# An 8-byte constant moves into another tile's slot: all later SBUF tiles of the first phase start 32 bytes lower

## The chip, the cores and the metric

One core of one Trainium2 chip runs the kernel. The metric is the device time of one execution in microseconds; the kernel before took 2728.22 us, the median of three runs (2727.66, 2728.22 and 2730.35). One more execution was recorded by the profiler, and all rows below are from it.

## What is computed

One layer of a hybrid decoder, on 4096 tokens of width 1024, in float32:

```
h    = rms_norm(x, norm_g)
u_lru, q, k, v, g_lr, q_xa, gate = split(h @ w_in)
y_lru = rg_lru(causal_conv4(u_lru), ...)          # gated linear recurrence, width 1024
y_gla = gla(q, k, v, g_lr @ w_g2 + b_g, ...)      # chunked linear attention, 4 heads
y_xa  = cross_attention(q_xa, rms_norm(mem) @ w_mem_kv)   # 256 memory tokens
y    = concat(y_lru, y_gla, y_xa) * silu(gate)    # width 2048
out  = rms_norm(x + y @ w_out, final_norm_g)
```

`b_g` is the bias of the decay logits of the linear attention; its negative, two numbers per partition, is the constant `nbg` of this case.

## The kernel before, in words

Matmuls need about float32 accuracy and are run in the type float32r. Each operand is split into a high and a low part of 4 bytes per element, and one product becomes three matmuls (`mm3`, lines 73 to 76): high by high, high by low, low by high. In `nc.tensor.matmul(o, a, b)` the second argument `a` is the stationary operand, a block of 128 by 128 that a weight load (PEld in the profile) brings into TensorE, and `b` is the moving operand, which streams past it. The page names them the other way round: `gate<-hh,whi` has `hh` moving and `whi` stationary.

Phase 1 works through the tokens in 4 blocks of 1024, each in two units of 512. `prep_gen` brings the normed activations of a unit into `hh` and `hl` (high and low part). `load_group` (line 102) loads a group of weights by DMA into `raw`, splits it on ScalarE (`whi`, line 110) and VectorE (`wlo`, line 111). `proj` (line 115) makes a projection: 8 slices of the contraction, three matmuls each, 24 matmuls of 512 columns, with the weights stationary and the activations moving. Names of the results are `gate`, `u`, `q` and `k`. The values `vp` (lines 475 to 477) are projected the other way: activations stationary, weights moving, 256 columns (272 where the low-rank decay factors ride along, with the first pair of heads). Between projections stand short pieces of the mixers: gates of the recurrence (`pr`, `pi`, lines 347 and 348), scores and output of the cross-attention (`sp`, lines 411 to 413; `ov`), and chunked attention in plain float32 (`pa`, `pk`, `pkv`, `po`, `pt`). Their steps are written as generators, one step per projection, so TensorE has projections to run while ScalarE and VectorE make its next operands. Every engine takes its instructions in the written order.

Phase 2 (from line 747) multiplies the gated outputs, read back from DRAM and split into `yh` and `yl` (stationary), by the output weights `wohi` and `wolo` (moving, 512 columns), adds the residual and norms. These are the matmuls `out`.

Where a tile lies in SBUF: pools are laid one behind the other in the order in which they are opened, each tile in its pool in the order in which it is made, and a tile's size per partition is rounded up to a multiple of 32 bytes. `cst` (constants of both phases, `hgn` among them), `small` and `hp` (`hh`, `hl`, later the first output weights) come first. Then follow the pools of phase 1: `c1` (constants, `nbg` among them), `xp`, `wp` (weights), `wk` and `wk1` (work tiles). When phase 1 ends its pools are closed, and those of phase 2 start where `c1` had started.

```
    hgn = cst.tile([P, 4], F32, name="hgn")                         # 16 bytes in a slot of 32
    nbg = c1.tile([P, 2], F32, name="nbg")                          # 8 bytes in a slot of 32
    ...
            nc.scalar.activation(out=rl[:, usl(u)], in_=z, func=AF.Relu, scale=-1.0, bias=nbg[:, p:p + 1])
```

Of the kernel before, what the change touches and what calls it, by code (L numbers as in the profile page):

```python
# [9 lines left out]
F32 = mybir.dt.float32  # L10
# [4 lines left out]
ALU = mybir.AluOpType  # L15
# [4 lines left out]
P = 128  # L20
# [6 lines left out]
EPS = 1e-6  # L27
LW = 1152

# columns of the packed per-channel parameters  # L30
C_CW, C_CB, C_BA, C_BI, C_LAM, C_BG, C_GN, C_NG, C_MG = 0, 32, 40, 48, 56, 64, 66, 70, 78
NPRM = 86
VW = 272
# [3 lines left out]
def hybrid_layer(ctx: ExitStack, tc: tile.TileContext, x, x_t, mem, mem_t, final_g,  # L37
                 w_lru, w_v0, w_oth, w_g2, w_mem, w_out, prm, out):
    nc = tc.nc
    T = x.shape[0]  # L40
# [21 lines left out]
    def col(c, n=1):  # L62
        return prm_sb[:, c:c + n]

    def rstd_of(ss, n, cols, tag, eng=None):
        """(ss/n + eps)^-0.5 on a [128, cols] tile."""
        ms = small.tile([P, cols], F32, tag=tag + "m", name=tag + "m")
        (eng or nc.gpsimd).tensor_scalar(out=ms, in0=ss, scalar1=1.0 / n, scalar2=EPS, op0=ALU.mult, op1=ALU.add)
        r = small.tile([P, cols], F32, tag=tag + "r", name=tag + "r")
        nc.gpsimd.tensor_tensor(out=r, in0=ms, in1=mhalf[:, :cols], op=ALU.pow)  # L70
        return r
# [11 lines left out]
    wk = p1.enter_context(tc.tile_pool(name="wk", bufs=2))  # L83
    wk1 = p1.enter_context(tc.tile_pool(name="wk1", bufs=1))

    # Work that waits for other engines is traced one step per projection tile, so that
    # the tensor engine has projections to run while its next operands are made.
    active = []

    def tick():  # L90
# [22 lines left out]
        return hi, lo  # L113

    def proj(o, wg, i, h, n=UNIT):
        """o[128 channels, n tokens] of channel tile i of a weight group."""
        hi, lo = wg
        hh, hl = h
        for kt in range(KT):
            s = slice(kt * P, (kt + 1) * P)  # L120
            mm3(o, hi[:, i, s], lo[:, i, s], hh[:, kt, :n], hl[:, kt, :n], kt == 0, kt == KT - 1)

    def prep_gen(src, src_t, tok0, n, c_g, hsel, spare=None, lean=False):
        """Normed activations of n token tiles, channel-major and split: x^T * g * rstd."""
        w = n * P
        nk = D // w
        t = slice(tok0 * P, tok0 * P + w)
        pend = []

        def load(i):  # L130
            xt = big(spare[i % len(spare)]) if lean else xp.tile([P, D], F32, tag="xt", name="xt", bufs=2)
            xt = xt.rearrange("p (k t) -> p k t", t=w)
            nc.sync.dma_start(out=xt, in_=src_t[i * nk * P:(i + 1) * nk * P, t].rearrange("(k p) t -> p k t", p=P))
            pend.append(xt)
        if lean:
            # the sums of squares from the transposed tiles alone
            for i in range(KT // nk):
                load(i)
            sq = xp.tile([P, D], F32, tag="x", name="sqs")[:, :w]
            for i in range(KT // nk):  # L140
                for k in range(nk):
                    if i + k == 0:
                        nc.scalar.activation(out=sq, in_=pend[i][:, k], func=AF.Square)
                        continue
                    s2 = wk.tile([P, w], F32, tag="t2", name="s2")
                    nc.scalar.activation(out=s2, in_=pend[i][:, k], func=AF.Square)
                    nc.vector.tensor_tensor(out=sq, in0=sq, in1=s2, op=ALU.add)
            ss = aux("ss")[:, :n]
            for c in range(n):
                nc.tensor.matmul(ss[:, c:c + 1], sq[:, c * P:(c + 1) * P], ones[:, 0:1], start=True, stop=True)  # L150
        else:
            ss = small.tile([P, n], F32, tag="xss", name="xss", bufs=3)
            for c in range(n):
                xr = big(spare[c % len(spare)]) if spare else xp.tile([P, D], F32, tag="x", name="x")
                nc.sync.dma_start(out=xr, in_=src[(tok0 + c) * P:(tok0 + c + 1) * P, :])
                junk = wk.tile([P, D], BF16, tag="t2", name="junk")
                nc.scalar.activation(out=junk, in_=xr, func=AF.Square, accum_out=ss[:, c:c + 1])
        r = rstd_of(ss, D, n, "x", nc.vector if lean else nc.gpsimd)
        yield 1
        if not lean:  # L160
            for i in range(2):
                load(i)
        yield 1
        pr = aux("rb")
        for c in range(n):
            nc.tensor.transpose(out=pr[:, c * P:(c + 1) * P], in_=r[:, c:c + 1].broadcast_to([P, P]),
                                identity=ident)
        rb = xp.tile([P, w], F32, tag="rb", name="rb")
        nc.scalar.copy(out=rb, in_=pr[:, :w])
        hh = hp.tile([P, KT, UNIT], F32R, tag="hh", name="hh")  # L170
        hl = hp.tile([P, KT, UNIT], F32R, tag="hl", name="hl")
        hsel((hh, hl))
        for i in range(KT // nk):
            xt = pend.pop(0)
            for k in range(nk):
                kt = i * nk + k
                nc.vector.scalar_tensor_tensor(out=xt[:, k], in0=xt[:, k], scalar=col(c_g + kt), in1=rb,
                                               op0=ALU.mult, op1=ALU.mult)
                nc.scalar.copy(out=hh[:, kt, :w], in_=xt[:, k])
                nc.vector.tensor_tensor(out=hl[:, kt, :w], in0=xt[:, k], in1=hh.bitcast(F32)[:, kt, :w],  # L180
                                        op=ALU.subtract)
            if not lean and i + 2 < KT // nk:
                load(i + 2)
            yield 1
# [19 lines left out]
    wm.append(load_group([w_mem[2], w_mem[3]], 1024))  # L204
    pending = [prep_x(0, 0), prep_x(0, 1)]

# [1 line left out]
    cmask = c1.tile([P, P], F32, name="cmask")  # L208
    make_upper_triangular(nc, cmask)
    attm = []  # L210
# [16 lines left out]
        nc.gpsimd.memset(t, 0.0)  # L227
        s_st.append(t)

    # c4 = 4 softplus(-lam) = 4 * (max(-lam, 0) + log1p(exp(-|lam|))), log1p(e) = 2 artanh(e / (2 + e))  # L230
    lam = col(C_LAM, 8)
    sc = cst.tile([P, 8, 8], F32, name="sc")
    e_ = sc[:, 0, :]
# [24 lines left out]
    nc.gpsimd.tensor_scalar(out=nba, in0=col(C_BA, 8), scalar1=-1.0, scalar2=None, op0=ALU.mult)  # L258
    hbi = cst.tile([P, 8], F32, name="hbi")
    nc.gpsimd.tensor_scalar(out=hbi, in0=col(C_BI, 8), scalar1=0.5, scalar2=None, op0=ALU.mult)  # L260
    hgn = cst.tile([P, 4], F32, name="hgn")
    nc.gpsimd.tensor_scalar(out=hgn, in0=col(C_GN, 4), scalar1=0.5, scalar2=None, op0=ALU.mult)
    nbg = c1.tile([P, 2], F32, name="nbg")
    nc.gpsimd.tensor_scalar(out=nbg, in0=col(C_BG, 2), scalar1=-1.0, scalar2=None, op0=ALU.mult)

    # low-rank decay path: the second factor stacked as [hi, lo, hi] to meet [hi, hi, lo] of the first
    gt = c1.tile([P, 4, 96], F32, name="gt")
    nc.gpsimd.memset(gt, 0.0)
    w2raw = wk1.tile([96, 256], F32, tag="ulo", name="w2raw")
# [2 lines left out]
    nc.scalar.copy(out=w2, in_=w2raw)  # L272
    nc.vector.tensor_tensor(out=w2[32:64, :], in0=w2raw[32:64, :], in1=w2.bitcast(F32)[32:64, :], op=ALU.subtract)

# [1 line left out]
    km_hi = c1.tile([P, 4, 256], F32R, name="km_hi")  # L276
    km_lo = c1.tile([P, 4, 256], F32R, name="km_lo")
    vm_hi = c1.tile([P, 2, 512], F32R, name="vm_hi")
# [5 lines left out]
    def silu_gate(wg, i, h, sg, u):  # L284
# [1 line left out]
        proj(g, wg, i, h)  # L286

        def post():
            # 2 silu(g) = (1 + tanh(g / 2)) g; what it multiplies carries the half
            nc.scalar.activation(out=sg[:, usl(u)], in_=g, func=AF.Tanh, scale=0.5)  # L290
            nc.vector.scalar_tensor_tensor(out=sg[:, usl(u)], in0=sg[:, usl(u)], scalar=1.0, in1=g,
                                           op0=ALU.add, op1=ALU.mult)
# [5 lines left out]
                          in_=y.rearrange("p (s t) -> p s t", t=P))  # L298

    class Group:  # L300
        """A pair of projection tiles; unit(u) yields after each projection."""

        def __init__(self, b, j, wg):
            self.b, self.j, self.wg = b, j, wg
# [5 lines left out]
    class Lru(Group):  # L310
        def setup(self):
            self.sg = self.rr = None
            # the last units are not held up for one another
            self.eager = self.b == nblk - 1 and self.j >= 6

        def unit(self, u, h):
# [10 lines left out]
        def post(self, u, o):  # L327
# [26 lines left out]
            if u < NU - 1 and not self.eager:  # L354
# [1 line left out]
            yield 1  # L356
            yield 1
            w = usl(u) if self.eager else slice(0, BLK)
            # 2 sigmoid(z) = exp(min(z, 0)) (1 + tanh(|z| / 2)), as exact in the lower tail as in the upper
            nc.scalar.activation(out=rr[:, w], in_=rr[:, w], func=AF.Tanh, scale=0.5)  # L360
            nc.scalar.activation(out=aa[:, w], in_=aa[:, w], func=AF.Exp, scale=-1.0)
            nc.vector.scalar_tensor_tensor(out=rr[:, w], in0=rr[:, w], scalar=1.0, in1=aa[:, w],
                                           op0=ALU.add, op1=ALU.mult)
            # log a = -c4 * 2 r; 1 - a^2 = tanh(c4 * 2 r) * (1 + a^2)
            nc.scalar.activation(out=aa[:, w], in_=rr[:, w], func=AF.Exp, scale=c4n[:, j:j + 1])
            nc.scalar.activation(out=rr[:, w], in_=rr[:, w], func=AF.Tanh, scale=c4[:, j:j + 1])
            for v in range(NU):
# [82 lines left out]
    gla_lr = {}  # L450

    class GlaV(Group):
        """Values, token-major; with the first pair of heads come the low-rank decay factors."""

        def setup(self):
            gla[self.j].clear()
# [53 lines left out]
                yield 1  # L510

    def gla_decay(p):
        """exp(+-(c - m)) with c the decay summed over 128 tokens and m its value at the midpoint."""
        gr = gla_lr["gr"]
        az, rl = big("r"), big("a")
        for u in range(NU):
# [115 lines left out]
                    store_y(self.b, 8 + 2 * p + hd, sg)  # L632
            yield 1

# [1 line left out]
    kinds = {"L": Lru, "X": Xa, "V": GlaV, "G": GlaG, "Q": GlaQ}  # L636

    def srcs(k, n):
# [16 lines left out]
        if i < len(flat) and i not in loaded:  # L655
            loaded[i] = load_group(*srcs(*flat[i][1:]))

    # memory keys and values, projected while the first tokens are normed
    def mem_post(ct, o):
        if ct < 4:  # L660
            nc.scalar.copy(out=km_hi[:, ct, :], in_=o[:, :256])
# [30 lines left out]
            tick()  # L692
    load_next(1)

    # output weights: the first 8 row tiles take the place of the activations of the last units
    wo = {}

    def wo_split(ct, raw, hi, lo):
# [45 lines left out]
        tick()  # L744
    p1.close()

# [1 line left out]
    yp = ctx.enter_context(tc.tile_pool(name="yp", bufs=2))  # L748
    rp = ctx.enter_context(tc.tile_pool(name="rp", bufs=2))
    w2a = ctx.enter_context(tc.tile_pool(name="w2a", bufs=1))  # L750
# [131 lines left out]
```

## Time and profile before

| | |
|---|---|
| runs | 2727.66, 2728.22, 2730.35 us |
| span of the profiled execution | 2731.1 us |
| TensorE busy (matmul) | 2696.2 us, 99% of the span |
| VectorE, ScalarE busy | 1382.1 us (51%), 1157.5 us (42%) |
| granted TensorE clock, mean | 0.998 of full speed |
| first projection, first matmul of phase 2 | about 62 us, about 2022 us into the span |

The page gives the span, from the first to the last instruction, and no other time of that execution; the span is 2.9 us (0.1%) above the median of the runs. A matmul's duration in the trace holds its way through the pipeline, so neighbours overlap: the pace of TensorE is read from the distance of two starts, not from a duration.

### The profile page before, as it was taken

To read this page: it belongs to the slowest core of one execution; us is meant where nothing else is said; L and a number is where in the kernel's file an instruction comes from. 1 tells how busy PE (TensorE), PEld (TensorE's weight loads), DVE (VectorE), ACT (ScalarE), POOL (GpSimd) and SP (SyncE) were. 2 spreads that over 40 slices of the span, in tenths; PEclk is the share of its full clock that TensorE was granted. 3 is DMA by queue.
4 is the path that set the end of the run, shared out by engine and by line. 5 is a ranking of instruction groups with operands and counts; after the bars stand their busy time and mean duration, and the time that the engine had idled before them with its cause. 6 is when DMAs were issued, how large, how long until landed. Compare 5 with 4: busy or idle time off the path is not lost.

```text
span 2731.1 us, 32855 instructions
## 1 busy us (share of the span) xinstructions
PE 2696.2 (99%) x13338; PEld 2249.0 (82%) x13338; DVE 1382.1 (51%) x2349; ACT 1157.5 (42%) x1802; POOL 88.7 (3%) x197
## 2 busy tenths in 40 slices
PE   7999999999999999999999999999999999999998
PEld 6888888888888878888887888888877888888887
DVE  6466546656664566666455756554573222222221
ACT  6355534644554465356436636543472111111110
POOL 2000000000000000000000000000000000000000
PEclk9999999999999999999999999999999999999999
DMA  8211212331212134112213312121243232222221
GB/s 273 66 59 57 62 58 66 123 104 52 71 54 64 51 118 127 56 58 64 64 49 104 101 51 76 54 70 41 66 164 137 93 106 102 101 93 93 93 93 62
DMA packets 119928, 231.64 MB, mean 85 GB/s; under 512 B 6528, under 2 KB 73184, under 8 KB 115680
## 3 DMA queue, kind: packets, MB, share of 16 engines
q1 hardware_dynamic: 119776, 229.54, 26.0%
q8 instruction: 104, 1.70, 0.3%
q14 instruction: 48, 0.39, 0.0%
HBM read 179.19 MB, written 50.33 MB: 84 GB/s over the span
## 4 chain that ended last, share of the span: by engine, by line
PE 89%; DVE 4%; DMA 4%; ACT 3%; issue 1%; POOL 0%; SPq 0%; DVEq 0%; POOLq 0%; ACTq 0%
PE out L75 8%; PE out L76 8%; PE out L74 8%; PE gate L74 8%; PE gate L75 8%; PE gate L76 8%; PE u L76 4%; PE u L75 4%; PE u L74 4%; PE q L74 3%; PE q L76 3%; PE q L75 3%; DMA x<-in_x 2%; PE vp L477 2%; PE vp L476 2%; PE vp L475 2%
## 5 line engine op out<-in xcount | busy, mean ns | idle before, releaser
L74 PE MATMUL gate<-hh,whi 128*128 128x512 f32 x1024 | 406.9, 397 | 0.0
L76 PE MATMUL gate<-hh,wlo 128*128 128x512 f32 x1024 | 405.0, 396 | 0.0
L75 PE MATMUL gate<-hl,whi 128*128 128x512 f32 x1024 | 405.0, 396 | 0.0
L75 PE MATMUL out<-wolo,yh 128*128 128x512 f32 x1024 | 398.8, 389 | 1.8 <-DVE wolo L706 1.5
L74 PE MATMUL out<-wohi,yh 128*128 128x512 f32 x1024 | 398.1, 389 | 1.0 <-ACT wohi L705 1.0
L76 PE MATMUL out<-wohi,yl 128*128 128x512 f32 x1024 | 398.4, 389 | 0.0
L111 DVE TENSOR_TENSOR wlo<-raw,whi 128x1024 fp32r<-128x1024 f32 (+2 forms) x152 | 191.5, 1281 | 222.0 <-ACT whi L110 185.9
L776 DVE TENSOR_TENSOR xr<-xr,out 128x512 f32<-128x512 f32 x64 | 43.9, 687 | 444.7 <-PE out L76 444.7
L76 PEld LDWEIGHTS gate<-hh,wlo 128*128 128x128 f32 x1024 | 192.3, 188 | 46.5
L74 PEld LDWEIGHTS gate<-hh,whi 128*128 128x128 f32 x1024 | 192.4, 188 | 46.4 <-issue 1.5
L110 ACT CAST whi<-raw 128x1024 fp32r<-128x1024 f32 (+2 forms) x152 | 162.5, 1096 | 157.6 <-PE gate L75 99.5
L75 PEld LDWEIGHTS gate<-hl,whi 128*128 128x128 f32 x1024 | 192.4, 188 | 44.7
L75 PEld LDWEIGHTS out<-wolo,yh 128*128 128x128 f32 x1024 | 192.2, 188 | 43.1 <-DVE wolo L706 2.7
L74 PEld LDWEIGHTS out<-wohi,yh 128*128 128x128 f32 x1024 | 192.1, 188 | 41.9 <-ACT wohi L705 2.0
L76 PEld LDWEIGHTS out<-wohi,yl 128*128 128x128 f32 x1024 | 192.2, 188 | 39.8
L74 PE MATMUL u<-hh,whi 128*128 128x512 f32 x512 | 206.6, 403 | 0.0
L75 PE MATMUL u<-hl,whi 128*128 128x512 f32 x512 | 202.4, 395 | 0.0
L76 PE MATMUL u<-hh,wlo 128*128 128x512 f32 x512 | 202.3, 395 | 0.0
L333 DVE SCALAR_TENSOR_TENSOR uc<-u,prm_sb,uc 128x511 f32<-128x511 f32 (+2 forms) x192 | 143.0, 745 | 75.2 <-ACT uc L330 74.7
L759 ACT CAST yh<-yr 128x2048 fp32r<-128x2048 f32 x32 | 61.2, 1912 | 257.7 <-PE out L75 256.4
L778 ACT ACTIVATE j<-xr 128x512 bf16<-128x512 f32 x64 | 40.0, 625 | 305.0 <-DVE xr L776 305.0
L74 PE MATMUL q<-hh,whi 128*128 128x512 f32 x384 | 152.6, 397 | 0.0
(219 smaller groups left out, 4977.0 us busy)
## 6 DMA issues: line engine op xcount, KB each, us to landing
raw<-in_w_oth SPq DMA_DIRECT2D x72, 512.0 KB, 3.8
raw<-in_w_lru SPq DMA_DIRECT2D x64, 576.0 KB, 3.9
yr<-y_d SPq DMA_DIRECT2D x32, 1024.0 KB, 5.2
xt<-in_x_t SPq DMA_DIRECT2D x32, 512.0 KB, 3.7
y_d<-sg SPq DMA_DIRECT2D x32, 512.0 KB, 3.8
y_d<-i SPq DMA_DIRECT2D x32, 512.0 KB, 3.2
xr<-in_x SPq DMA_DIRECT2D x32, 512.0 KB, 3.5
out<-xr SPq DMA_DIRECT2D x31, 512.0 KB, 4.1
```

The lines of the kernel that those rows point to most:

```text
L74: nc.tensor.matmul(o, w_hi, r_hi, start=start, stop=False)
L75: nc.tensor.matmul(o, w_hi, r_lo, start=False, stop=False)
L76: nc.tensor.matmul(o, w_lo, r_hi, start=False, stop=stop)
L110: nc.scalar.copy(out=hi[:, i, :width], in_=raw[:, :width])
L111: nc.vector.tensor_tensor(out=lo[:, i, :width], in0=raw[:, :width], in1=hi.bitcast(F32)[:, i, :width], op=ALU.subtract)
L333: nc.vector.scalar_tensor_tensor(out=uc[:, d:UNIT], in0=o[:, 0:UNIT - d], scalar=w, in1=uc[:, d:UNIT], op0=ALU.mult, op1=ALU.add)
L475: nc.tensor.matmul(o, hh, wh, start=kt == 0, stop=False)
L476: nc.tensor.matmul(o, hh, wl, start=False, stop=False)
L477: nc.tensor.matmul(o, hl, wh, start=False, stop=kt == KT - 1)
L759: nc.scalar.copy(out=yh, in_=yr)
L776: nc.vector.tensor_tensor(out=xt[:, c], in0=xt[:, c], in1=o[n], op=ALU.add)
L778: nc.scalar.activation(out=junk, in_=xt[:, c], func=AF.Square, accum_out=ss[:, n:n + 1])
```

## The change

`nbg` is no longer a tile of `c1`. `hgn` grows from 4 to 6 numbers per partition (24 bytes, still in its slot of 32), and `nbg` is the last two of them. The readers of `nbg` read the same values from there. Elsewhere the diff only drops comments; line numbers stay.

```
-    hgn = cst.tile([P, 4], F32, name="hgn")
-    nc.gpsimd.tensor_scalar(out=hgn, in0=col(C_GN, 4), scalar1=0.5, scalar2=None, op0=ALU.mult)
-    nbg = c1.tile([P, 2], F32, name="nbg")
+    hgn = cst.tile([P, 6], F32, name="hgn")
+    nc.gpsimd.tensor_scalar(out=hgn[:, 0:4], in0=col(C_GN, 4), scalar1=0.5, scalar2=None, op0=ALU.mult)
+    nbg = hgn[:, 4:6]
     nc.gpsimd.tensor_scalar(out=nbg, in0=col(C_BG, 2), scalar1=-1.0, scalar2=None, op0=ALU.mult)
```

The instructions of all five engines are the same in number, kind and order. What differs is where tiles start. Byte addresses within a partition, and the rest on division by 64:

| tiles | before | rest | after | rest |
|---|---|---|---|---|
| `hh` (two buffers), `hl` (two) | 20928, 37312, 53696, 70080 | 0 | the same | 0 |
| `qz0`, `qz1`, `attm0` to `3`, `s_st0`, `s_st1`, `ident`, `st` | | 0 | the same | 0 |
| `gt`, `w2`, `km_hi`, `km_lo`, `vm_hi`, `vm_lo` | 100832 ... 115680 | 32 | 32 less | 0 |
| `xt`, `rb`, `glr`, `x` | 119776 ... 134112 | 32 | 32 less | 0 |
| `whi` (two), `wlo` (two) | 138208, 147424, 156640, 165856 | 32 | 32 less | 0 |
| `raw`, `sg`, `t2`, `i`, `r`, `a`, `uc`, `ulo`, `uhi` | 175072 ... 227296 | 32 | 32 less | 0 |
| phase 2: `yh`, `yl`, `wohi`, `wolo`, `xr`, ... | 86464 ... 215488 | 0 | the same | 0 |

The slices that matmuls read in these tiles start at multiples of 64 bytes from the tile's start (512 bytes for a block of 128, 1024 and 1088 bytes for the values' weights).

## Rows read from the trace of the kernel before

**Rows 1.** The page: engines' busy time, and the granted clock in 40 slices
```profile
span 2731.1 us, 32855 instructions
PE 2696.2 (99%) x13338; PEld 2249.0 (82%) x13338; DVE 1382.1 (51%) x2349; ACT 1157.5 (42%) x1802; POOL 88.7 (3%) x197
PEclk9999999999999999999999999999999999999999
```

**Rows 2.** Groups by line: output and inputs, form, count | busy us, mean ns | idle us
```profile
L75 PE MATMUL gate<-hl,whi 128*128 128x512 f32 x1024 | 405.0, 396 | 0.0
L75 PE MATMUL u<-hl,whi 128*128 128x512 f32 x512 | 202.4, 395 | 0.0
L75 PE MATMUL q<-hl,whi 128*128 128x512 f32 x384 | 151.8, 395 | 0.0
L75 PE MATMUL k<-hl,whi 128*128 128x512 f32 x128 | 50.6, 396 | 0.0
L76 PE MATMUL out<-wohi,yl 128*128 128x512 f32 x1024 | 398.4, 389 | 0.0
L76 PE MATMUL ov<-phi,vm_lo 128*128 128x512 f32 x64 | 24.9, 390 | 0.0
L476 PE MATMUL vp<-wlo,hh 128*128 128x256 f32 x256 | 71.5, 279 | 0.0
L476 PE MATMUL vp<-wlo,hh 128*128 128x272 f32 x256 | 74.3, 291 | 0.0
L412 PE MATMUL sp<-km_lo,uhi 128*128 128x256 f32 x128 | 35.9, 283 | 0.0
```

**Rows 3.** Timeline, TensorE, projections q and k: start us, duration us, instruction
```profile
366.12 0.40 PE L74 MATMUL q<-hh,whi 128*128 128x512 f32 x1
...
388.28 0.39 PE L76 MATMUL k<-hh,wlo 128*128 128x512 f32 x1
```

**Rows 4.** Timeline, TensorE, phase 2
```profile
2299.65 0.39 PE L74 MATMUL out<-wohi,yh 128*128 128x512 f32 x1
...
2321.86 0.39 PE L76 MATMUL out<-wohi,yl 128*128 128x512 f32 x1
```

**Rows 5.** Windows: us, busy us (count) of each engine, clock, DMA share, GB/s
```profile
660.00:680.00 20.00, 20.00 (x87) 16.14 (x86) 17.27 (x29) 18.04 (x24) 0.00 (x0) 1.00 0.38 113
840.00:860.00 20.00, 20.00 (x87) 16.14 (x86) 3.16 (x4) 3.19 (x5) 0.00 (x0) 1.00 0.23 73
2300.00:2320.00 20.00, 20.00 (x90) 16.57 (x89) 4.87 (x5) 3.25 (x5) 0.73 (x2) 1.00 0.27 98
```

**Rows 6.** Timeline, TensorE, cross-attention output and recurrence gates
```profile
231.30 0.39 PE L75 MATMUL ov<-plo,vm_hi 128*128 128x512 f32 x1
...
233.57 0.39 PE L76 MATMUL pi<-uhi,wlo 128*128 128x512 f32 x1
```

**Rows 7.** Timeline, TensorE, scores of the cross-attention
```profile
197.20 0.28 PE L412 MATMUL sp<-km_lo,uhi 128*128 128x256 f32 x1
...
198.40 0.28 PE L413 MATMUL sp<-km_hi,ulo 128*128 128x256 f32 x1
```

**Rows 8.** Timeline, TensorE, values of 272 columns, then of 256
```profile
73.39 0.29 PE L475 MATMUL vp<-whi,hh 128*128 128x272 f32 x1
...
85.28 0.29 PE L477 MATMUL vp<-whi,hl 128*128 128x272 f32 x1
...
326.45 0.28 PE L475 MATMUL vp<-whi,hh 128*128 128x256 f32 x1
...
343.13 0.28 PE L477 MATMUL vp<-whi,hl 128*128 128x256 f32 x1
```

**Rows 9.** Timeline, TensorE, a wait at the end of a block
```profile
497.28 0.39 PE L411 MATMUL sp<-km_hi,uhi 128*128 128x256 f32 x1 [1.28 <-ACT uhi L403]
```

**Rows 10.** Timeline, ScalarE, sums of squares of the next tokens
```profile
979.34 1.06 ACT L157 ACTIVATE junk<-x 128x1024 bf16<-128x1024 f32 x1 [1.83 <-DMA x<-in_x]
...
984.10 1.06 ACT L157 ACTIVATE junk<-x 128x1024 bf16<-128x1024 f32 x1 [3.60 <-DMA x<-in_x]
```

**Rows 11.** Window at the turn from block 2 to block 3
```profile
1020.00:1060.00 40.00, 39.97 (x229) 34.76 (x228) 38.14 (x65) 28.14 (x48) 0.00 (x0) 1.00 0.50 152
```

**Rows 12.** Groups by line: the same operation on tiles of both phases
```profile
L111 DVE TENSOR_TENSOR wlo<-raw,whi 128x1024 fp32r<-128x1024 f32 x80 | 95.8, 1222 | 84.7 <-ACT whi L110 48.7 <-PE pT L434 35.5
L706 DVE TENSOR_TENSOR wolo<-wraw,wohi 128x1024 fp32r<-128x1024 f32 x8 | 9.8, 1224 | 7.3 <-ACT wohi L705 7.3
L705 ACT CAST wohi<-wraw 128x1024 fp32r<-128x1024 f32 x8 | 8.3, 1044 | 8.4 <-DMA wraw<-in_w_out 8.3
```

## The prediction

> **What bounds the kernel now.** I read the page's engine table first: TensorE is busy for 99% of the span at the full granted clock, VectorE for 51% and ScalarE for 42% [rows 1]. So the time is the number of matmuls times the distance between two starts, plus a few waits. The groups by line give the counts and a first oddity: the same kind of matmul, 512 columns with a full stationary block, takes 395 to 396 ns in a projection of phase 1 and 389 ns in phase 2, and 390 ns in the `ov` of phase 1 [rows 2]. These durations overlap, so I took distances of starts from the timeline.
>
> - Projections `q` and `k`: 96 matmuls in a row, 95 distances from 366.12 to 388.28 us, 22.16 / 95 = 233.3 ns [rows 3].
> - Phase 2: 99 matmuls in a row, 98 distances from 2299.65 to 2321.86, 22.21 / 98 = 226.6 ns [rows 4].
> - `ov`, `pr`, `pi` one behind the other, in phase 1: 10 distances from 231.30 to 233.57, 227 ns [rows 6].
>
> The 6.6 ns between the first and the other two are not disturbance by other engines: two stretches of projections, one with VectorE and ScalarE busy 17.27 and 18.04 of 20 us, the other 3.16 and 3.19, hold the same 87 matmuls, and phase 2 holds 90 [rows 5]. Nor is it the phase, since `ov` to `pi` lie in the middle of phase 1. What differs is the place of the two operands, which the table of addresses in the section on the change gives. In a projection the moving operand (`hh`, `hl`) starts at a multiple of 64 bytes and the stationary one (`whi`, `wlo`) 32 bytes past one. In phase 2 both start at a multiple. In `ov`, `pr` and `pi` both start 32 past one. So, by these rows, 512 columns cost 226.6 ns when both operands have the same rest modulo 64 (a larger power of two up to 256 would fit as well), and 233.3 ns when the rests differ.
>
> With 256 columns the order is the other way round. `sp`, both at rest 32: 10 distances in 1.20 us, 120.0 ns [rows 7]. `vp`, moving at rest 32, stationary at 0: 143 distances in 16.68 us, 116.6 ns; with 272 columns 95 distances in 11.89 us, 125.2 ns [rows 8]. At 2.4 GHz, the granted clock in all these stretches, 512 columns alone are 213.3 ns and 256 are 106.7 ns; equal rests add 13.3 ns to both, unequal ones 19.9 ns to 512 columns and 9.9 ns to 256.
>
> **The change part by part.** No instruction is added, removed or moved. After it every matmul of phase 1 has both operands at rest 0, which is the case of phase 2.
>
> 1. Projections: 3 x (1024 + 512 + 384 + 128) = 6144 matmuls [rows 2], all back to back on the path that sets the end. Each comes 233.3 - 226.6 = 6.6 ns sooner (22.16/95 less 22.21/98): -40.6 us. If rests had no part in it: 0.
> 2. `ov`, `pr`, `pi`: 9 groups of 64, one of them shown [rows 2], 576 matmuls. Settled they already run at 227 ns [rows 6]; those next to a projection are still at its pace. Between 0 and 576 x 6.6 ns = 3.8 us; I take -1, since the group's mean of 390 ns is near the 389 of phase 2.
> 3. Values: 768 matmuls of 256 columns and 768 of 272 (three lines of 256 each [rows 2]). No row shows such a matmul with both at rest 0. The nearest is `sp`, equal rests and 256 columns, at 120.0: +3.4 ns each, +2.6 us; for 272 columns 113.3 + 13.3 = 126.6, +1.4 ns each, +1.1 us. The other end: if the added time grows with the columns, 226.6 x 256/512 = 113.3 and 226.6 x 272/512 = 120.4, that is -2.5 and -3.7 us. I take the first, being the nearer row.
> 4. `sp`: both operands move together, rest 32 to rest 0: 0, as phase 2 and `ov` show for 512 columns. At the other end 113.3 ns, 384 x 6.7 = -2.6 us.
> 5. VectorE, ScalarE, DMA: the same subtraction takes 1222 ns on phase 1's tiles at rest 32 and 1224 ns on phase 2's at rest 0 [rows 12]. I cost them at nothing; TensorE's work covers them anyway.
> 6. Waits that become late. TensorE arrives sooner at places where others set the time. At the end of a block ScalarE stands in its order behind sums of squares that wait for DMA through a single buffer, 4.8 us apart [rows 10], and TensorE waits 1.28 us for it [rows 9]. At the turn of a block VectorE is busy 38.14 of 40 us [rows 11]; what TensorE gains there, some 160 projections x 6.6 ns = 1.1 us, it gives back. With some 20 us in front of the first place (85 matmuls, 0.6 us) this is 1.7 us a turn, three turns: +5 us. It is at least 0; if the stretches that other engines pace are twice as long, +10.
>
> Sum: -40.6 - 1 + 2.6 + 1.1 + 5 = -32.9 us. Against the profiled span 2731.1 that is 2698.2; the runs' median lies 2.9 us below that span, so 2695.3, say 2695 us.
>
> **The rule that speaks against it.** Two kinds of rows say that starts matter to TensorE [rows 3, 4]. The Trainium skill says otherwise in two places. *SBUF — State Buffer*, under "Door 1: The DMA port swizzle", gives SBUF lines of 16 bytes; both layouts start on one. *TensorE: Matmul & The Clock Gate*, under "Step-by-step", says of weight loads: "Loading the next tile's weights doesn't steal SBUF read bandwidth from the running matmul." By these two step 1 would be 0 and the time the one of before, the first of the rivals below. The trace does not agree, as to equal distances: 233.3 against 226.6 ns.
>
> **The rivals.**
>
> - *No change.* The two paces come from something else that is fixed in the program, such as which regions of SBUF the operands lie in (`hh` low, `whi` high), and stay. For it: the cause is inferred from three kinds of pairs. Against: `pr` takes the very tile `whi` as stationary and runs at 227 [rows 6]. Step 3 would go with it: 2728 us.
> - *Short matmuls gain too.* Rest 0 is better than equal rests at 32, and the added time goes with the columns: steps 3 and 4 at their other ends. -40.6 - 1 - 2.5 - 3.7 - 2.6 + 5 = -45.4, less 2.9: 2682.8 us. For it: nothing but that 0/0 at 256 columns is not in the trace. Against: `sp` at 120.0, and 0/0 and 32/32 alike at 512.
> - *Equal rests collide, slower than before.* In the values equal rests are the dearer case, 120.0 against 116.6. If that, 3.4 ns for each stationary block loaded beside a running matmul, is what alignment does in phase 1, and the 226.6 of phase 2 has another cause, then 6144 x 3.4 = +20.9 us and +3.7 for the values: 2728 + 25 = 2753 us. It decides if a projection's distance rises above 233.3 at all. Against: `ov` to `pi`, equal rests, 512 columns, 227.
> - *The change does not do what it says.* `hgn` with 24 bytes still fits its slot of 32, so `hh` stays and all behind `nbg` goes down by 32; I leave it no chance of its own.
>
> **How the numbers follow.** The forecast has 0.70, with its own range of 2689 to 2704 (step 6 between 0 and +10, step 2 between its ends, step 3 as taken). Short matmuls gain too: 0.18. No change: 0.08. Collision: 0.04. The range 2681 to 2706 takes in the forecast and the second rival, with 2 us beyond each, and leaves out the other two and the tails, some 0.15. What a measurement of this kernel can tell from no change is about 0.2%, 5.5 us. Faster by more: the first two, 0.88. Within: 0.08. Slower: 0.04.
>
> **What would show it.** In the profile after, the timeline of `q` and `k` should show 226.6 ns from start to start, and the groups of the projections 389 ns instead of 395 to 396. `vp` should show 120 and 126.6 ns (113.3 and 120.4 for the second rival), `sp` 120.0 as before. The waits of lines 411 and 477 should be a little longer. Phase 2 should begin some 33 us earlier and last as long. The prediction is wrong at its first step if the projections stay at 233.3 ns; it is wrong in step 6 if they go to 226.6 and phase 2 begins less than 25 us earlier.

## Result and profile after

The changed kernel took 2699.27 us, the median of four runs (2698.56 to 2699.65), against 2728.01 for four runs of before: ratio 0.9892, 95% interval [0.9878, 0.9906], 28.7 us less. The forecast was 2695 us. The profiled execution has a span of 2697.9 us and lies 1.75 us below the time of its own run.

The page after, its engine table and the clock, for [rows 1]:

```profile
span 2697.9 us, 32855 instructions
PE 2660.9 (99%) x13338; PEld 2249.6 (83%) x13338; DVE 1381.3 (51%) x2349; ACT 1156.6 (43%) x1802; POOL 92.4 (3%) x197
PEclk9999999999999999999999999999999999999999
```

The instructions are the same in number, the clock is the same, and the work of VectorE and ScalarE is within 1 us of before. Only the busy time of TensorE falls, by 35.3 us. The groups by line, for [rows 2] (busy us, mean ns | idle us):

```profile
L75 PE MATMUL gate<-hl,whi 128*128 128x512 f32 x1024 | 398.6, 389 | 0.0
L75 PE MATMUL u<-hl,whi 128*128 128x512 f32 x512 | 199.6, 390 | 0.0
L75 PE MATMUL q<-hl,whi 128*128 128x512 f32 x384 | 149.7, 390 | 0.0
L75 PE MATMUL k<-hl,whi 128*128 128x512 f32 x128 | 49.8, 389 | 0.0
L76 PE MATMUL out<-wohi,yl 128*128 128x512 f32 x1024 | 398.4, 389 | 0.0
L476 PE MATMUL vp<-wlo,hh 128*128 128x256 f32 x256 | 72.4, 283 | 0.0
L476 PE MATMUL vp<-wlo,hh 128*128 128x272 f32 x256 | 74.6, 292 | 0.0
L111 DVE TENSOR_TENSOR wlo<-raw,whi 128x1024 fp32r<-128x1024 f32 x80 | 95.7, 1222 | 85.9 <-ACT whi L110 51.5 <-PE pT L434 34.1
```

The projections, at 395 to 396 ns before, now take the 389 to 390 of phase 2; the values of 256 columns went up from 279 to 283; VectorE's subtraction, whose three tiles all moved, stays at 1222. The timeline of `q` and `k`, for [rows 3] (start us, duration us):

```profile
360.54 0.39 PE L74 MATMUL q<-hh,whi 128*128 128x512 f32 x1
...
362.62 0.39 PE L74 MATMUL q<-hh,whi 128*128 128x512 f32 x1
...
382.12 0.39 PE L76 MATMUL k<-hh,wlo 128*128 128x512 f32 x1
```

95 distances in 21.58 us are 227.2 ns, where before it was 233.3. The stretch begins right behind a short piece of another kind (`z`): its first 9 distances, up to 362.62, average 232 ns, the other 86 average 226.7. Phase 2 begins 31.9 us earlier, at 1989.64 instead of 2021.59 us:

```profile
1989.64 0.39 PE L74 MATMUL out<-wohi,yh 128*128 128x512 f32 x1
```

And the wait at the end of a block, for [rows 9], with the window at the turn of the block, for [rows 11]:

```profile
489.55 0.39 PE L411 MATMUL sp<-km_hi,uhi 128*128 128x256 f32 x1 [1.73 <-ACT uhi L403]
```
```profile
1005.00:1045.00 40.00, 39.95 (x232) 35.32 (x231) 38.18 (x66) 27.82 (x47) 0.00 (x0) 1.00 0.51 155
```

The wait grew from 1.28 to 1.73 us: TensorE gets there 8.2 us sooner than before, what ScalarE makes for it (`uhi`) only 7.7 us. VectorE is as full at the turn as before.

### The profile page after: what moved, and what is told of

The parts are those of the page before. It is cut to its first block, busy times and chain, and to the rows that moved or that the text cites. A ratio compares the mean times of both kernels' runs of the same rounds, so it can differ in the third digit from the quotient of the medians.

```text
span 2697.9 us, 32855 instructions
## 1 busy us (share of the span) xinstructions
PE 2660.9 (99%) x13338; PEld 2249.6 (83%) x13338; DVE 1381.3 (51%) x2349; ACT 1156.6 (43%) x1802; POOL 92.4 (3%) x197
## 2 busy tenths in 40 slices
DMA packets 119928, 231.64 MB, mean 86 GB/s; under 512 B 6528, under 2 KB 73184, under 8 KB 115680
## 3 DMA queue, kind: packets, MB, share of 16 engines
q1 hardware_dynamic: 119776, 229.54, 26.2%
## 4 chain that ended last, share of the span: by engine, by line
PE 86%; DMA 4%; DVE 4%; ACT 4%; issue 1%; POOL 1%; SPq 0%; DVEq 0%; POOLq 0%; ACTq 0%
PE out L75 8%; PE out L74 8%; PE out L76 8%; PE gate L74 7%; PE gate L75 7%; PE gate L76 7%; PE u L75 4%; PE u L76 4%; PE u L74 4%; PE q L75 3%; PE q L74 3%; PE q L76 3%; DMA x<-in_x 2%; PE vp L477 2%; PE vp L476 2%; PE vp L475 2%
## 5 line engine op out<-in xcount | busy, mean ns | idle before, releaser
L74 PE MATMUL gate<-hh,whi 128*128 128x512 f32 x1024 | 400.6, 391 | 0.0
L76 PE MATMUL gate<-hh,wlo 128*128 128x512 f32 x1024 | 398.8, 389 | 0.0
L75 PE MATMUL gate<-hl,whi 128*128 128x512 f32 x1024 | 398.6, 389 | 0.0
```

Source lines behind the costliest of these rows:

```text
L74: nc.tensor.matmul(o, w_hi, r_hi, start=start, stop=False)
L75: nc.tensor.matmul(o, w_hi, r_lo, start=False, stop=False)
L76: nc.tensor.matmul(o, w_lo, r_hi, start=False, stop=stop)
```

## Experiments

**Back to the old places, without the old tile.** An unused tile of 8 bytes lies where `nbg` lay.

```
     nbg = hgn[:, 4:6]
+    pad = c1.tile([P, 2], F32, name="pad")
+    nc.gpsimd.memset(pad, 0.0)
```

> The changed kernel with an unused 8-byte tile where nbg lay, so that all tiles of phase 1 are back at their old addresses (rest 32), while nbg stays in hgn's slot. Theory: the place of the other tiles is all; projections 233.3 ns from start to start, values 116.6, time as before the change, 2728 us. Rival: reading nbg from the other tile or pool saves the time; then it stays near 2699 us.

Measured: 2728.41 us, ratio to before 1.0 [0.9991, 1.0008], and in the groups by line

```profile
L75 PE MATMUL gate<-hl,whi 128*128 128x512 f32 x1024 | 405.0, 396 | 0.0
L478 PE MATMUL vp<-wlo,hh 128*128 128x256 f32 x256 | 71.5, 279 | 0.0
```

So the whole gain is in where the other tiles lie; where `nbg` is read from has no part in it. This kernel's trace, with a span of 2726.6 us, is also a second look at the layout of before.

**Both operands at rest 32.** 32 unused bytes ahead of the pool of `hh` and `hl`; every later tile of both phases moves up with it.

```
+    pad = ctx.enter_context(tc.tile_pool(name="pad", bufs=1)).tile([P, 2], F32, name="pad")
+    nc.gpsimd.memset(pad, 0.0)
     hp = ctx.enter_context(tc.tile_pool(name="hp", bufs=2))
```

> The changed kernel with 32 unused bytes ahead of the activations' pool: everything from hh on, in phase 1 and phase 2, moves up by 32 bytes, so that both operands of nearly every matmul have rest 32. Theory (equal rests): projections and phase 2 at 226.7 ns, values at 120.0, time as after the change, 2699 us (2696 to 2702). Rival (multiples of 64 count by themselves): projections at 233.3 or more and phase 2 slower too, 3072 matmuls x 6.6 ns = 20 us above before at the most, 2728 to 2748 us.

Measured: 2699.34 us, ratio 0.9894 [0.9881, 0.9908], as the change itself.

```profile
L75 PE MATMUL gate<-hl,whi 128*128 128x512 f32 x1024 | 398.7, 389 | 0.0
L76 PE MATMUL out<-wohi,yl 128*128 128x512 f32 x1024 | 398.4, 389 | 0.0
```

No operand of the projections or of phase 2 starts at a multiple of 64 here, and nothing is lost. The multiple of 64 is not what counts; how the two operands stand to each other is.

**Work tiles alone at rest 32.**

```
+    pad = p1.enter_context(tc.tile_pool(name="pad", bufs=1)).tile([P, 2], F32, name="pad")
+    nc.gpsimd.memset(pad, 0.0)
     wk = p1.enter_context(tc.tile_pool(name="wk", bufs=2))
```

> The changed kernel with 32 unused bytes ahead of the work tiles alone: whi, wlo, raw and the constants stay at rest 0 like hh, the work tiles of ScalarE and VectorE (sg, i, r, a, t2, uc, uhi, ulo) are back at rest 32. Theory: projections stay at 226.7 and values at 120; ov, pr and pi now have unequal rests, at most 576 x 6.6 ns = 3.8 us dearer, sp 384 x 2 to 3.4 ns cheaper: 2699 to 2703 us. Rival: part of the gain came from ScalarE's, VectorE's or the DMAs' accesses to work tiles; then that part of the 28.7 us is lost, 2710 us or more.

Measured: 2704.37 us, ratio 0.9913 [0.99, 0.9927], 5.1 us above the changed kernel and 1.4 above the range expected, far from the rival's 2710.

```profile
L75 PE MATMUL gate<-hl,whi 128*128 128x512 f32 x1024 | 399.2, 390 | 0.0
L76 PE MATMUL ov<-phi,vm_lo 128*128 128x512 f32 x64 | 25.4, 397 | 0.0
```

`ov`, whose moving operand is off by 32 again, rises from 390 to 397 ns; `pr` and `pi`, the first matmul of `pr` aside, rise from between 390 and 392 ns to between 394 and 396. Summing the distances of starts over phase 1 gives +3.1 us for these three, as expected, -0.4 for `sp` (0.8 to 1.3 less was expected), and +2.3 that was not expected at all: `gate`, `u` and `q` right behind such a piece take longer to come down to 227 ns than in the changed kernel (230.6 instead of 227.2 ns over the first 8 behind `pi`).

**The pair by itself.** A kernel with nothing but matmuls, 36 in a row for each setting:

```
i, j = 512 * (k % 4) + m // size, 128 * (k % 8) + s // size
nc.tensor.matmul(o[:, :n], b[:, j:j + P], a[:, i:i + n], start=k == 0, stop=k == rep - 1)
```

> A kernel of its own that only measures: groups of 36 matmuls on 128 partitions, each with a weight load, with the moving operand m bytes and the stationary operand s bytes past a multiple of 512 bytes; 512, 448, 384, 272, 256 and 128 columns; float32r, and a few groups in bfloat16. Its output is not the layer's. Theory (equal rests modulo 64): from start to start 226.7 ns at 512 columns for (m, s) = (0,0), (0,64), (0,128), (64,0), (32,32), (16,16), (4,4); 233.3 for (0,32), (32,0), (0,96). At 256 columns 120.0 for equal rests and 116.7 for (32,0), at 272 126.7 and 125.2. Rests other than 32 (4, 8, 16, 48) are not in the traces so far. Rival A (a larger modulus, 128 or 256): (0,64) and (64,0) run at 233.3 as well. Rival B (each operand must start at a multiple of 64): (32,32), (16,16) and (4,4) are slower than 226.7. Rival C (lines of 16 bytes): all offsets that are multiples of 16 run alike, only 4 and 8 are dearer.

Distances of starts in ns, mean of the last 27 of each group, float32r; the pairs are (moving, stationary), in bytes past a multiple of 512:

| columns | (0,0) | (32,32) | (0,32) | (32,0) | (0,64) | (64,0) | (0,128) | (16,16) | (4,4) |
|---|---|---|---|---|---|---|---|---|---|
| 512 | 226.7 | 226.7 | 233.4 | 233.3 | 233.3 | 228.9 | 232.4 | 231.1 | 239.2 |
| 256 | 120.0 | 120.0 | 118.3 | 116.6 | 113.3 | 117.8 | 118.7 | 116.6 | 122.2 |

128 columns took 111.6 to 111.7 at every offset, 384 columns 173.3 at all four tried, 448 columns 202.6 to 206.7. 272 columns took 125.1 for (0,0), not the 126.7 expected for equal places, and 125.0 to 125.6 for the other three. The bfloat16 groups of 512 columns took 216 ns at every offset. In the timeline of this kernel, `can` is (32,32), `cao` (16,16), `ccl` and `cco` bfloat16 with (0,0) and (32,0):

```profile
140.85 8.34 PE L53 MATMUL can<-mov,sta 128*128 128x512 f32 x36
149.02 8.49 PE L53 MATMUL cao<-mov,sta 128*128 128x512 f32 x36
...
387.62 7.94 PE L53 MATMUL ccl<-movb,stab 128*128 128x512 bf16 x35
...
410.94 7.93 PE L53 MATMUL cco<-movb,stab 128*128 128x512 bf16 x36
```

The pace of the projections and of phase 2 is reproduced to 0.1 ns with no other engine at work, and (32,32) at 226.7 speaks against rival B. But (0,64) at 233.3 contradicts the theory: equal rests modulo 64 are not enough. It also speaks against rival C, since 16, 32 and 64 are all multiples of 16 and do not run alike. Rival A fits better, though not wholly: (64,0), at 228.9, lies between its two paces.

**The step by 32.** The same kernel, the difference of the two places from 0 to 480 in steps of 32.

> The second measuring kernel, of the same make as the first (its output is not the layer's): 36 matmuls in a row in float32r, the stationary operand s bytes further than the moving one, s from 0 to 480 in steps of 32, with the moving one at 0 and at 32, at 512 and at 256 columns; some groups again behind a group of 128 columns, to see whether what ran before matters. The first measuring kernel gave 226.7 ns for equal places but 233.3 for a difference of 64 and about 232 for 128, against the rule of equal rests modulo 64. Theory now (equal places modulo 512, the step of the stationary blocks): at 512 columns only a difference of 0 gives 226.7, all other steps of 32 give 229 to 234, whatever ran before. Rival (the pace is a state that the start fixes, not the place): the repeated groups differ from the first ones by 3 ns and more at the same s. At 256 columns a difference of 64 gave 113.3 and 0 gave 120.0: expected again, also with the moving operand at 448 and the stationary at 0.

The difference is the stationary operand's place less the moving one's. The timeline, 512 columns, moving operand at 0; `caa` is a difference of 0, `cab` 32, `cac` 64, `cae` 128, `cag` 192, `cai` 256, `caj` 288:

```profile
31.38 8.33 PE L56 MATMUL caa<-mov,sta 128*128 128x512 f32 x36
39.55 8.55 PE L56 MATMUL cab<-mov,sta 128*128 128x512 f32 x36
47.94 8.56 PE L56 MATMUL cac<-mov,sta 128*128 128x512 f32 x36
56.34 8.59 PE L56 MATMUL cad<-mov,sta 128*128 128x512 f32 x36
64.77 8.53 PE L56 MATMUL cae<-mov,sta 128*128 128x512 f32 x36
73.14 8.55 PE L56 MATMUL caf<-mov,sta 128*128 128x512 f32 x36
81.53 8.40 PE L56 MATMUL cag<-mov,sta 128*128 128x512 f32 x36
89.77 8.56 PE L56 MATMUL cah<-mov,sta 128*128 128x512 f32 x36
98.16 8.33 PE L56 MATMUL cai<-mov,sta 128*128 128x512 f32 x36
106.33 8.55 PE L56 MATMUL caj<-mov,sta 128*128 128x512 f32 x36
```

From one group's start to the next: 8.17 us for 0, 8.37 to 8.43 for 32 to 160 and 224, 8.24 for 192, and 8.17 again for 256. The settled distances are 226.7 at 0 and 256, 228.9 at 192 and 448, 232.4 to 234.3 at the rest. With the moving operand at 32 they are the same to 0.1 ns at the same difference. So, for places that are multiples of 32, the difference modulo 256 decides at 512 columns (the 228.9 of (64,0) above is this row's 192); the 512 that I expected was wrong too. The groups repeated behind 128 columns came back within 0.4 ns: at 512 columns what ran before leaves no mark on the settled pace. At 256 columns the place alone does not fix the pace: a difference of 64 ran at 113.3 ns in the first measuring kernel (first fence, `cax`) and, with 448 for the moving operand, here (`ccw`), but at 117.8 in this kernel's row of differences (`cbi`), although both kernels lay out their tiles alike and `cax` and `cbi` read the same addresses. What picks one of the two paces no run shows.

```profile
199.82 4.25 PE L53 MATMUL cax<-mov,sta 128*128 128x256 f32 x36
203.91 4.48 PE L53 MATMUL cay<-mov,sta 128*128 128x256 f32 x36
```
```profile
302.85 4.42 PE L56 MATMUL cbh<-mov,sta 128*128 128x256 f32 x36
307.11 4.40 PE L56 MATMUL cbi<-mov,sta 128*128 128x256 f32 x36
311.35 4.39 PE L56 MATMUL cbj<-mov,sta 128*128 128x256 f32 x36
...
529.51 4.25 PE L56 MATMUL ccw<-mov,sta 128*128 128x256 f32 x36
533.60 4.42 PE L56 MATMUL ccx<-mov,sta 128*128 128x256 f32 x36
```

**64 and 256 bytes in the kernel itself.** Half of the projections get their weights 16 (then 64) columns further in the tile.

```
+            nc.scalar.copy(out=hi[:, i, off:off + width], in_=raw[:, :width])
...
+            loaded[i] = load_group(*srcs(*flat[i][1:]), off=16 if flat[i][1] in "XGQ" else 0)
```

> The changed kernel with the weights of the groups X, G and Q (two projections each, with 1024 of 1152 columns used) 16 columns, 64 bytes, further in their tile; the rest modulo 64 stays 0, the difference to the activations becomes 64. Half of the projections, 3072 matmuls. Rule of the prediction (rests modulo 64): all projections at 226.7 ns, 2699 us. Theory after the first measuring kernel (places must agree modulo 512): these 3072 at about 233.3, 3072 x 6.6 ns = 20 us more, about 2718 us (2710 to 2720).

> As the kernel with the weights of X, G and Q 64 bytes further, but 256 bytes (64 columns of their tile): the place of weights and activations then differs by 256. Theory after the two measuring kernels (places modulo 256 decide at 512 columns): projections at 226.7 ns as after the change, 2699 us (2696 to 2702). Rival (modulo 512, the step of the stationary blocks): the 3072 projections at 233.3, 2717 us as with 64 bytes.

Measured: 64 bytes 2716.71 us, ratio 0.9959 [0.9946, 0.9973]; 256 bytes 2700.69 us, ratio 0.9895 [0.988, 0.991]. With 64 bytes (first fence) `u`, left alone, keeps its 390 ns, `q` is back at 395, and `gate`, half of it moved, at 392; with 256 (second fence) `q` has 390:

```profile
L75 PE MATMUL gate<-hl,whi 128*128 128x512 f32 x1024 | 401.7, 392 | 0.0
L75 PE MATMUL u<-hl,whi 128*128 128x512 f32 x512 | 199.7, 390 | 0.0
L75 PE MATMUL q<-hl,whi 128*128 128x512 f32 x384 | 151.8, 395 | 0.0
```
```profile
L75 PE MATMUL q<-hl,whi 128*128 128x512 f32 x384 | 149.8, 390 | 0.0
```

So 64 bytes for half of the projections cost 17.4 us, against the rule of the prediction, and 256 bytes nothing that the runs can tell. All operands of the projections lie at multiples of 64 in both. That the change brings the tiles to multiples of 64 is thus a coincidence: its 32 bytes also made `whi`, `wlo` and the work tiles agree with `hh` modulo 512 (138176 - 20928 = 229 x 512).

**The values at another difference.** The same edit with `off=112` for V1 alone.

> The changed kernel with the weights of the second values group (V1, 768 matmuls of 256 columns, weights moving) 448 bytes further in their tile, all else as after the change. The measuring kernels gave 113.3 ns with the moving operand at 448 and the stationary at 0, and 117.8 in another run of groups with the same difference, against 120.0 for equal places. Theory: vp of 256 columns at 113.3 or 117.8 instead of 119.9, 768 x 6.6 = 5.1 us or 768 x 2.1 = 1.6 us less: 2694 to 2697.7 us. Rival: the values' pace depends on the mix of high and low parts, which the measuring kernels don't have, and stays at 120: 2699 us.

Measured: 2697.59 us, ratio 0.9884 [0.9868, 0.9901]; `vp` of 256 columns settled at 117.8, not 113.3 ns, 1.65 us less over 768 matmuls. It is clearly faster than the kernel before; against the changed kernel, 1.7 us (0.06%) is less than the runs can tell apart, only the trace shows it.

```profile
L476 PE MATMUL vp<-wlo,hh 128*128 128x256 f32 x256 | 71.9, 281 | 0.0
```

## Why the prediction came out

The time lies in the range, and what carries the forecast was right: the place of the two operands relative to each other sets the pace of the 512-column matmuls. The rule by which the prediction judged that place, equal rests modulo 64, was wrong and gave the right pace by luck (last point below), and several terms were off in size. The second trace of the old layout (2726.6 us) against the one after (2697.9) gives, by summing distances of starts between the first and the last projection, to a few tenths of a us:

| step | forecast, us | traces, us |
|---|---|---|
| 1 projections | -40.6 | -36.8 |
| 2 `ov`, `pr`, `pi` | -1 | -0.9 |
| 3 values, 256 and 272 columns | +2.6, +1.1 | +2.5, +0.5 |
| 4 `sp` | 0 | -0.1 |
| 6 waits | +5 | +3.0, and +1.0 in the transposes of `pT` |
| between first and last projection | -32.9 | -30.8 |

- *Step 1* took the settled 6.6 ns for all 6144. The mean over all of them went from 233.2 to 227.2, 6.0 ns: in the new layout the first 10 or so projections behind a piece of another kind run slower, 230.8 ns for the first two and 227 for the ninth and tenth on average, before they settle at 226.7. In the old layout they run at 232.6 to 233.6 from the start, so the rows of before could not show it.
- *Step 3* for 272 columns assumed equal places for every slice. The slices are 1088 bytes apart, so their difference to the activations goes through 0, 64, 128 and 192 modulo 256 in the new layout (32, 96, 160 and 224 in the old one); the matmuls took 125.9 instead of 126.6 ns, against 125.2 before. And adding the 13.3 ns of 256 columns to 272 was wrong by itself: the first measuring kernel gave 125.1 ns with all places equal. For 256 columns the value taken from `sp`, 120.0, was exact (119.9).
- *Step 5* held: no group of VectorE or ScalarE changed, and the work tiles at rest 32 cost only matmul time.
- *Step 6*: TensorE's waits for ScalarE's `uhi` at line 403 rose from 3.2 us in the trace of before to 5.0, at the place that was forecast; with all others the loss is 4.0 us against the 5 forecast.
- *What lies outside the table.* The forecast is the runs' median less 32.9 us; measured are 28.7 less, the same as between the spans of these two traces. Of the 4.2 us between, 2.1 lie in the table. The other 2.1 lie where the prediction gave the layout no part: in the trace after, the first projection comes 1.4 us later than in the repetition of the old layout (TensorE waits 11.9 instead of 10.4 us for `xr` from GpSimd), and the time from the start of phase 2 to the end is 0.8 us longer. Two traces of the old layout differ by as much there, 1.6 and 2.1 us, so this is taken as scatter between executions. It is also why the span of before, 2731.1, misleads: in every later run the time lies some 1.75 us above its span, not below it, so that execution was itself some 4.6 us longer than the usual one, and its trace differs from the one after by 33.2 us. That this nearly equals the 32.9 of the forecast is chance.
- *The prediction's own range.* Its 2689 to 2704 do not follow from the ends it names: step 6 between 0 and +10 and step 2 between its ends give 2687.5 to 2701.3.
- *The rivals.* No change and collision fell with the 227.2 ns of `q` and `k`. That short matmuls gain too fell with 119.9. And the rule by which I argued, modulo 64, is wrong as a rule: 64 bytes of difference cost as much as 32. It gave the right number, by luck, because the change makes the difference a multiple of 512; the rows of before could not tell 64 from 256, which the prediction said in half a sentence and then did not carry on.

## What to carry to other kernels

Where float32r matmuls of 512 columns run back to back with a weight load each, compare the start-to-start distance of every group with the best group of the same shape: 226.7 against 233.3 ns was 2.8% of a projection and made 1.6% of phase 1 (30.8 of 1958.7 us), with no idle time to point to it. Then look at the difference of the two operands' addresses modulo 256, and give both pools starts that agree; here 32 bytes did it. At 256 columns agreement is not the best place: 120.0 ns against 113.3 to 119.9 for most other differences. Take a change that is summed from distances off the runs' median, and repeat a trace before its span is trusted to a few us: two executions of one layout lay 4.6 us apart.

## What the hardware showed beyond that

- With equal places float32r carries 13.3 ns (32 cycles at 2.4 GHz, the granted clock being 1.00 in these stretches) more than its columns at 512, 384, 320 and 256 columns, but 15.9 at 448, 16.5 at 480 and 11.8 at 272. bfloat16 takes 216 ns at 512 and 109.2 at 256 columns, at all five pairs of offsets tried. The Trainium skill (*TensorE: Matmul & The Clock Gate*, "Wait — 56ns, not 53.3ns?") gives the columns at 2.4 GHz and about 2.5 ns; bfloat16 agrees, float32r does not.
- What in TensorE or SBUF makes the difference modulo 256 matter was not settled. That moving operand and weight load compete for the same place of SBUF is a guess; a run with one weight load for several matmuls would test it, and none was made. bfloat16 and 128 columns of float32r (111.6 ns throughout) are indifferent. Offsets that are no multiple of 32 follow another rule: (16,16) ran at 231.1 and (16,48) at 226.7 ns.
